# The last two tiles of an embedding's gate, multiplied before or after a conditional branch

## The chip, the cores and the metric

The kernel runs on one core of a Trainium2 chip. The core has five engines with instruction streams of their own: TensorE (PE: matrix products and transposes; PEld is its weight load), VectorE (DVE), ScalarE (ACT), GpSimd (POOL) and SyncE (SP), which here issues most of the DMA transfers. The metric is the time of one execution on the device, in microseconds (us). Before the change it is 3113.56 us, the median of 3 runs (3111.11 to 3114.87).

## The reference

The program computes two blocks one after the other on 512 tokens of 1024 features. The first block (attention, retention and a feed-forward network, with modulation) isn't touched. The second has two layers, and each ends with the part that matters here:

```python
for i in range(DEPTH):
    ...                                   # mixers, w_out
    h = layer_norm(DN_ALPHA * h + mix, ln1_g[i], ln1_b[i])
    y_moe = hier_moe(h, moe_wgc[i], moe_bgc[i], moe_wgf[i], moe_bgf[i],
                     moe_w1[i], moe_w3[i], moe_w2[i])
    y_ple = jax.nn.sigmoid(h @ ple_wg[i] + ple_bg[i]) * (p[i] @ ple_wp[i])
    h = layer_norm(DN_ALPHA * h + y_moe + y_ple, ln2_g[i], ln2_b[i])
```

`hier_moe` picks for each token one of 4 groups and 2 of its 4 experts; an expert is `(silu(t @ w1) * (t @ w3) * gate) @ w2` with 256 inner features. `y_ple`, the embedding, is a 1024 x 1024 product with a sigmoid, times a product of a 256-feature input `p`.

## The kernel before

Activations lie feature by feature: `x[:, m, token]` is feature tile m (128 features) of 512 tokens, and there are 8 tiles. Every product of full precision is made of three (`mm3`, L365): the weights and the activations are each split into a high part (ScalarE, L308) and a low part (VectorE, L309), and high x high, high x low and low x high are added up in one accumulator (L368, L369, L370). Weights are loaded by SyncE into stage slots (`stage`, L284) of two rings: `UPS` names the slots of the even pools, `DOWNS` those of the odd one.

`second_half` (L2648) is the end of a layer. The embedding's tiles 0 to 5 are multiplied and added early (`ple_g`, L2251, is the product, the sigmoid on ScalarE L2258 and the multiplication on VectorE L2259; `ple_add`, L2262, adds it to `ALPHA * x`, L2264). Then come the experts (`experts`, L2582). Tokens are gathered in blocks of 128: blocks 0 to 15 are the first 128 tokens of each expert, and blocks 16 to 22 take what experts have beyond that. For each block GpSimd gathers rows (`gather`, L2487), TensorE transposes them and multiplies up (`up`, L2540) and down (`down`, L2566); the result is evicted in two halves, by ScalarE (L2574) and VectorE (L2575), each scaled by the gate, and scattered by GpSimd to `ydram` (L2576). Which tokens a block beyond 16 holds is worked out by `list_further` (L2474): VectorE marks positions (L2373), TensorE multiplies (L2483), VectorE makes the indices (L2380 to L2387).

How many of blocks 17 to 22 are needed is known only at run time. `further` (L2616) loads the count into a register on every engine (L2618) and runs blocks 17 and 18 in an `If` (L2619), with blocks 19 to 22 in a second `If` inside it (L2621). A scheduler orders the instructions of each engine, but only within a stretch without branches: what is written before an `If` stays before it, what is written behind stays behind, on all engines. On a branch that isn't taken each engine counts what it has skipped, so that others who wait for it can go on.

Behind the branch SyncE loads the experts' results back token by token (`load`, L2628, 8 loads `rt`, L2636). `TokenNorm` (L712) makes the layer norm: `rows` (L715) transposes x to tokens (TensorE L722; copies ACT L726 and DVE L724), `tokens` (L729) adds the two loaded rows (L735, L736 with its sum), squares (ACT L738), takes the root on GpSimd (L384), scales (L743, two halves) and transposes back (TensorE L746, ACT L747). There are four token tiles t of 128; a half hf is 256 tokens, two of them. `gen` (L749) then makes the high and low parts of the new activations. In layer 0 the next layer's first projection (`Front.first`, L1859, tiles `wl`) follows, with panels loaded by `Front.panels` (L1855); in layer 1 the output is written.

In the kernel before, tiles 6 and 7 of the embedding (`ple(6, w67, UPS)`) and the list of block 17 (`list_further(1)`) are written behind block 16 and ahead of the branch.

Of the kernel before, what the change touches and what calls it, by code (L numbers as in the profile page):

```python
# [462 lines left out]
HS = (slice(0, 256), slice(256, 512))  # L463
# [248 lines left out]
class TokenNorm(LayerNorm):  # L712


    def rows(self, t):  # L715

        net, nc = self.net, self.net.nc
        X = self.pool.tile([128, D], F32, name=net.nm("xr"), tag="xr", bufs=4)
        for j in range(2):
# [3 lines left out]
            if j:  # L723
                nc.vector.tensor_copy(X[:, 512:], tr.rearrange("p m d -> p (m d)"))  # L724
            else:
                nc.scalar.activation(X[:, :512], tr.rearrange("p m d -> p (m d)"), AF.Copy)  # L726
        return X

    def tokens(self, t, X, r):  # L729

        net, nc, pool = self.net, self.net.nc, self.pool
        vt = nc.vector
        small = lambda tag: pool.tile([128, 1], F32, name=net.nm(tag), tag=tag, bufs=2)
        mean, var = small("tmean"), small("tvar")
        vt.tensor_tensor(X, X, r[0], op=OP.add)  # L735
        vt.scalar_tensor_tensor(X, X, 0.0, r[1], op0=OP.add, op1=OP.add, accum_out=mean)  # L736
        vt.tensor_scalar(mean, mean, -1.0 / D, None, op0=OP.mult)
        nc.scalar.activation(r[1], X, AF.Square, bias=mean, accum_out=var)  # L738
        vt.tensor_scalar(var, var, 1.0 / D, EPS2, op0=OP.mult, op1=OP.add)
        rstd = net.rsqrt(pool, var, 1)  # L740
        for j in range(2):
            cs = slice(512 * j, 512 * j + 512)
            vt.tensor_scalar(X[:, cs], X[:, cs], mean, rstd, op0=OP.add, op1=OP.mult)  # L743
            tr = self.sp.tile([128, 4, 128], F32, name=net.nm("tr"), tag="tr", bufs=2)
            for m in range(4):
                nc.tensor.transpose(tr[:, m], X[:, (4 * j + m) * 128:(4 * j + m + 1) * 128], net.ident)  # L746
            nc.scalar.activation(self.x[:, 4 * j:4 * j + 4, t * 128:(t + 1) * 128], tr, AF.Copy)  # L747
# [1444 lines left out]
UPS, DOWNS = slice(0, None, 2), slice(1, 2)  # L2192


class Moe:
# [34 lines left out]
    def small(self, name, *shape, dt=F32):  # L2230
        return self.mp.tile([128] + list(shape), dt, name=self.net.nm(name), tag="m_" + name)
# [253 lines left out]


    def gather(self, b):  # L2487
        if b >= 18:
            self.list_further(b - 16)
        xg = self.mp.tile([128, D], F32, name=self.net.nm("xg"), tag="xg", bufs=2)  # L2490
        self.net.nc.gpsimd.indirect_dma_start(out=xg, out_offset=None, in_=self.hd[:, :],
                                              in_offset=bass.IndirectOffsetOnAxis(ap=self.idx[:, b, 0:1], axis=0))
        return xg
# [147 lines left out]
def lnpools(net):  # L2641
    es = ExitStack()
    pool = es.enter_context(net.pool(net.nm("ln"), side="right"))
    sp = es.enter_context(net.pool(net.nm("ln_ps"), space=PSUM, side="right"))
    return es, pool, sp


def second_half(net, i, sides, hh, hl, lns, last):  # L2648

    moe = Moe(net, i, hh, hl)  # L2650
    pw = {m2: moe.ple_p(m2) for m2 in (0, 2)}
    pan = [net.cpanel(moe.wg[:, :, m2 * 128:m2 * 128 + 256], 8, 256) for m2 in (0, 2)]
    lt, sg = [], {}
    for hf in range(2):
        sides[hf].finish()
        if hf:
            lns.close()
            ms = ExitStack()
            ms.enter_context(net.more(0, 2))
        lt = moe.logits(hf)  # L2660
        for m in range(4):
            sg = moe.ple_g(m, pan[m // 2][m % 2], pw[m // 2 * 2][m % 2], HS[hf])
            if m == 0:
                moe.logits_t(hf, lt)
                moe.rows(hf)
                if hf:
                    router = net.side(moe.route())
            moe.ple_add(m, sg, HS[hf])
    full = slice(0, S)

    def ple(m2, w, some=slice(None)):
        g = net.cpanel(moe.wg[:, :, m2 * 128:m2 * 128 + 256], 8, 256, some=some)
        for mm in range(2):
            moe.ple_add(m2 + mm, moe.ple_g(m2 + mm, g[mm], w[mm], full), full)

    ple(4, moe.ple_p(4), UPS)
    w67 = moe.ple_p(6)
    moe.pes.close()
    ms.enter_context(net.more(0, 2))
    w0 = moe.first_weights()  # L2680
    net.finish(router)
    lists = moe.lists()

    with ms:
        def beside(e):
            for _ in range(2 if 3 <= e < 9 else 1):
                next(lists, None)

        blocks = [(e, e, (lambda e=e: beside(e))) for e in range(16)]
        moe.experts(blocks + [(16, moe.further_expert(0), None)], w0)  # L2690
        moe.list_further(1)
        ple(6, w67, UPS)
        moe.further()
    lns, pool, _ = lnpools(net)
    out = [TokenNorm(net, pool, moe.sp, net.x, hs, None if last else hh, hl, gname=f"l2g{i}", bname=f"l2b{i}") for hs in HS]
    pans = []
    rows = [moe.load(t) for t in range(4)]
    if not last:
        pans += Front.panels(net, i + 1, 512)
    X = [out[t // 2].rows(t) for t in range(4)]  # L2700
    for t in range(4):
        out[t // 2].tokens(t, X[t], rows[t])
        if t % 2:
            out[t // 2].start()
        if t == 3 and not last:
            pans += Front.panels(net, i + 1, 256)
    moe.es.close()
    return out, lns, pans


def second_block(net, stages, boundary):
# [15 lines left out]
    for i in layers:  # L2727
        front = Front(net, i, hh, hl)
        front.first(sides, pans)
        if i == 0:  # L2730
            net.tap("h_in0", net.x)
        lns.close()
        bs.close()
        front.second()
        front.mp2 = front.left.enter_context(net.pool(f"mixB{i}"))
        front.attention()
        bs.enter_context(net.more(3))
        lns, pool, sp = lnpools(net)
        sides = front.out_second(pool, sp, f"l1g{i}", f"l1b{i}")
        front.left.close()  # L2740
        if f"h1_{i}" in net.taps:
            for s in sides:
                s.finish()
            net.tap(f"h1_{i}", net.x)
        sides, lns, pans = second_half(net, i, sides, hh, hl, lns, i == layers[-1])
# [24 lines left out]
```

## Time and profile before

| what | us |
|---|---|
| median of 3 runs | 3113.56 |
| the profiled execution | 3106.33 |
| its span, first to last instruction | 3104.2 |
| layer 0: last block's down-products start | 2488.48 |
| layer 0: next layer's projection starts | 2526.86 |
| layer 1: last block's down-products start | 3060.32 |
| layer 1: last scaling starts | 3095.36 |

A row of a timeline gives the start from the span's begin, the duration, the engine, the line, the operation, the output and inputs by the program's names (without their numbers), the shape, how many instructions the row groups, and in brackets how long the engine was idle before and who released it. A name with a q (PEldq, DVEq) is an engine's queue, where branches and semaphores are handled. The granted clock (PEclk) is the share of TensorE's full clock that it was given.

### The profile page before, as it was taken

Reading aid. Unit: us, or ns where it says so; the run is one execution under the profiler, and the core shown is the slowest. Engines: PE = TensorE matmul, PEld = TensorE weight load, DVE = VectorE, ACT = ScalarE, POOL = GpSimd, SP = SyncE. Lnnn points to the kernel's source line nnn. Section 1 sums busy time; section 2 is a strip of 40 time slices with the busy share of each in tenths; the row PEclk is TensorE's granted clock in tenths of the full one; section 3 lists DMA queues with packets and bytes.
Section 4 is the critical chain, followed back from the end, with each engine's and each line's share of the span. In section 5 each row is a group of like instructions: output and inputs, shape, how many; then the busy total and the mean of one; then the engine's idle time right before and its main releaser. Section 6 shows DMA issues by size and latency. Waiting matters only on the chain. (4 is left out here: it accounts for less than half of the span.)

```text
span 3104.2 us, 42345 instructions
## 1 busy us (share of the span) xinstructions
PE 2939.8 (95%) x16384; PEld 2427.0 (78%) x16384; DVE 1902.0 (61%) x3557; ACT 1298.5 (42%) x2227; POOL 406.0 (13%) x389
## 2 busy tenths in 40 slices
PE   6999989999999999999999999999999988999995
PEld 5777779888888888888887788877876767787663
DVE  5566575545552664535465543669778766988865
ACT  3655563121212432323243322436555543656544
POOL 1112130000000200000020000221212212121220
PEclk8999999999999999999999999999999989999997
DMA  6121133324441222223133432231469944146993
GB/s 223 49 74 55 49 98 100 116 89 129 144 142 55 88 67 82 78 67 98 37 114 117 125 127 96 89 119 41 133 201 362 351 161 121 35 153 226 378 352 142
DMA packets 307875, 410.18 MB, mean 132 GB/s; under 512 B 16655, under 2 KB 248207, under 8 KB 307025
## 3 DMA queue, kind: packets, MB, share of 16 engines
q1 hardware_dynamic: 293840, 357.03, 35.0%
q0 software_dynamic: 13824, 50.34, 4.5%
q8 instruction: 133, 2.18, 0.3%
q14 instruction: 78, 0.63, 0.1%
HBM read 379.01 MB, written 28.31 MB: 131 GB/s over the span
## 5 line engine op out<-in xcount | busy, mean ns | idle before, releaser
L308 ACT ACTIVATE hi<-st 128x1024 fp32r<-128x1024 f32 (+1 forms) x420 | 432.7, 1034 | 691.9 <-PE ps L369 497.6
L309 DVE TENSOR_TENSOR lo<-st,hi 128x1024 fp32r<-128x1024 f32 (+1 forms) x420 | 510.5, 1219 | 233.9 <-ACT hi L308 222.5
L368 PE MATMUL ps<-hxh,hi 128*128 128x512 f32 (+1 forms) x1280 | 477.3, 374 | 2.5 <-DVE sg L828 0.8
L369 PE MATMUL ps<-hxl,hi 128*128 128x512 f32 (+1 forms) x1280 | 475.3, 372 | 0.5 <-DVE hxl L645 0.5
L370 PE MATMUL ps<-hxh,lo 128*128 128x512 f32 (+1 forms) x1280 | 475.0, 371 | 0.0
L368 PEld LDWEIGHTS ps<-hxh,hi 128*128 128x128 f32 x1280 | 241.9, 189 | 52.2 <-ACT sg L827 5.6
L370 PEld LDWEIGHTS ps<-hxh,lo 128*128 128x128 f32 x1280 | 242.0, 189 | 42.4 <-issue 1.2
L369 PEld LDWEIGHTS ps<-hxl,hi 128*128 128x128 f32 x1280 | 242.1, 189 | 41.2 <-issue 1.2
L368 PE MATMUL ps<-ah,hi 128*128 128x256 f32 (+1 forms) x592 | 200.5, 339 | 3.2 <-DVE x L774 1.6
L369 PE MATMUL ps<-al,hi 128*128 128x256 f32 (+1 forms) x592 | 198.5, 335 | 0.2 <-DVE al L378 0.2
L370 PE MATMUL ps<-ah,lo 128*128 128x256 f32 (+1 forms) x592 | 198.4, 335 | 0.0
L774 DVE SCALAR_TENSOR_TENSOR x<-ps,vecs,x 128x512 f32<-128x512 f32 (+1 forms) x136 | 84.4, 623 | 147.9 <-PE ps L370 147.8
L828 DVE TENSOR_TENSOR sg<-sg,ps 128x512 f32<-128x512 f32 (+1 forms) x70 | 40.1, 572 | 187.0 <-PE ps L370 186.3
L593 POOL TENSOR_TENSOR nacc<-nacc,nsq 128x256 f32<-128x256 f32 x56 | 49.4, 883 | 594.7 <-ACT nsq L592 593.5
L368 PEld LDWEIGHTS ps<-ah,hi 128*128 128x128 f32 x592 | 111.4, 188 | 19.0 <-DVE x L774 3.6
L2571 PE MATMUL py<-st,at 128*128 128x512 f32 x272 | 123.0, 593 | 1.7 <-DVE y L2575 1.2
L369 PEld LDWEIGHTS ps<-al,hi 128*128 128x128 f32 x592 | 111.5, 188 | 12.6 <-DVE al L378 0.4
L370 PEld LDWEIGHTS ps<-ah,lo 128*128 128x128 f32 x592 | 111.3, 188 | 12.6
L2545 PE MATMUL pa<-hi,xt 128*128 128x512 f32 x288 | 118.5, 412 | 0.5 <-ACT xt L377 0.5
L368 PE MATMUL ps<-hch,hi 128*128 128x256 f32 x416 | 117.7, 283 | 0.6 <-DVE mod L527 0.5
L369 PE MATMUL ps<-hcl,hi 128*128 128x256 f32 x416 | 117.2, 282 | 0.0
L370 PE MATMUL ps<-hch,lo 128*128 128x256 f32 x416 | 117.1, 282 | 0.0
(671 smaller groups left out, 7065.7 us busy)
## 6 DMA issues: line engine op xcount, KB each, us to landing
st<-moe_w_dram SPq DMA_DIRECT2D x136, 512.0 KB
st<-ffn_w_in_dram SPq DMA_DIRECT2D x44, 1024.0 KB
st<-moe_w_dram SPq DMA_DIRECT2D x34, 1024.0 KB
ast<-ada_w_dram SPq DMA_DIRECT2D x56, 512.0 KB
st<-ret_w_qkvg_dram SPq DMA_DIRECT2D x24, 1024.0 KB
st<-ffn_w_out_dram SPq DMA_DIRECT2D x24, 768.0 KB
st<-ada_w_dram SPq DMA_DIRECT2D x12, 1024.0 KB
st<-w_in_dram SPq DMA_DIRECT2D x12, 1024.0 KB
```

The costliest lines, as they stand in the source:

```text
L308: self.nc.scalar.activation(h, v, AF.Copy)
L309: self.nc.vector.tensor_tensor(l, v, h.bitcast(F32), op=OP.subtract)
L368: self.nc.tensor.matmul(ps, wh, xh, start=(i == 0), stop=False)
L369: self.nc.tensor.matmul(ps, wh, xl, start=False, stop=False)
L370: self.nc.tensor.matmul(ps, wl, xh, start=False, stop=(i == n - 1))
L593: nc.gpsimd.tensor_tensor(self.acc, self.acc, sq, op=OP.add)
L774: net.nc.vector.scalar_tensor_tensor(xm, p, self.gate[:, m:m + 1], xm, op0=OP.mult, op1=OP.add)
L828: nc.vector.tensor_tensor(sg, sg, pu, op=OP.mult)
L2545: nc.tensor.matmul(pa, th[:, k], wh, start=(k == 0), stop=False)
L2571: nc.tensor.matmul(py[:, n * 512:n * 512 + 512], at[:, f], w2[f][:, 0, n * 512:n * 512 + 512], start=(f == 0), stop=(f == 1))
```

## The change

The list of block 17 is made in `gather(17)`, so inside the branch, as the lists of blocks 18 to 22 already were. The gate weights of tiles 6 and 7 are loaded and split behind `further()`, and their products are made for each half of the tokens (256 columns) between the issue of the row loads and the transposes of that half. In layer 0 the load of the next layer's first two panels is written behind that instead of ahead of the transposes.

```diff
     def gather(self, b):
-        if b >= 18:
+        if b >= 17:
             self.list_further(b - 16)
...
         moe.experts(blocks + [(16, moe.further_expert(0), None)], w0)
-        moe.list_further(1)
-        ple(6, w67, UPS)
         moe.further()
+        g67 = net.cpanel(moe.wg[:, :, 768:1024], 8, 256, some=UPS)
     lns, pool, _ = lnpools(net)
...
     rows = [moe.load(t) for t in range(4)]
+
+    X = []
+    for hf, hs in enumerate(HS):
+        for mm in range(2):
+            moe.ple_add(6 + mm, moe.ple_g(6 + mm, g67[mm], w67[mm], hs), hs)
+        X += [out[hf].rows(t) for t in (2 * hf, 2 * hf + 1)]
     if not last:
         pans += Front.panels(net, i + 1, 512)
-    X = [out[t // 2].rows(t) for t in range(4)]
     for t in range(4):
         out[t // 2].tokens(t, X[t], rows[t])
```

The first place is SyncE's queue in layer 0. Before, ahead of the branch (`COMPARE_AND_BRANCH`), the panel of `ple_wg` stood among the down weights of the last blocks:

```order
L2515 DMA st_20962<-moe_w_2_dram 128x4x256
L284 DMA st_21115<-ple_wg_dram 128x8x256
L284 DMA st_20787<-moe_w_2_dram 128x2x1024
L284 DMA st_20871<-moe_w_2_dram 128x2x1024
L284 ISA
L284 DMA st_20965<-moe_w_2_dram 128x2x1024
L2619 COMPARE_AND_BRANCH
```

Three loads of weights and the whole branch stood behind it. Now, at the end of the same branch, it stands behind the branch's last instruction:

```order
L284 DMA st_21687<-moe_w_2_dram 128x2x1024
L2621 UNCONDITIONAL_BRANCH x2
L2619 UNCONDITIONAL_BRANCH
L284 DMA st_21814<-ple_wg_dram 128x8x256
L2636 DMA rt_21832<-ydram_18602 128x1024
L2636 DMA rt_21834<-ydram_18602 128x1024
```

It has moved past the branch, directly ahead of the eight row loads.

The second place is TensorE's queue at the start of that branch in layer 0. Before, the gate products of tiles 6 and 7 (`ps`, 512 columns) stood last ahead of the branch:

```order
L368 MATMUL ps_21154<-hxh_15866,hi_21121 128x512
L369 MATMUL ps_21154<-hxl_15867,hi_21121 128x512
L370 MATMUL ps_21154<-hxh_15866,lo_21122 128x512
L2618 TENSOR_LOAD exi_20375
L2619 COMPARE_AND_BRANCH
```

Now the last down-products (`py`) stand there:

```order
L2571 MATMUL py_21069<-st_20871,at_21039 128x512 x4
L2561 MATMUL tr_21078<-kident_69,act_21066 128x128 x2
L2571 MATMUL py_21083<-st_20965,at_21081 128x512 x4
L2618 TENSOR_LOAD exi_20375
L2619 COMPARE_AND_BRANCH
```

The gate products are gone from here; they stand behind the branch, after twelve of the transposes of L722.

The third place is VectorE's queue in the token stage of layer 0. Before, the low-part splits of the next layer's panels (`lo`) stood behind the last scaling (`nry_22050`, the fourth token tile):

```order
L758 TENSOR_SCALAR x<-x,vec 128x256
L739 TENSOR_SCALAR tvar_22044<-tvar_22044 128x1
L743 TENSOR_SCALAR xr_21955<-xr_21955,tmean_22043,nry_22050 128x512 x2
L309 TENSOR_TENSOR lo_21909<-st_21906,hi_21908 128x1024
L309 TENSOR_TENSOR lo_21913<-st_21906,hi_21912 128x1024
```

Now two of them stand between the two scalings of the first token tile (`nry_22033`), with the copies of later tiles, and ahead of the third tile's first sum (`L735`); two more stand ahead of the third tile's scaling:

```order
L2264 SCALAR_TENSOR_TENSOR x<-x,sg_21957 128x256
L737 TENSOR_SCALAR tmean_22026<-tmean_22026 128x1
L735 TENSOR_TENSOR xr_21919<-xr_21919,rt_21836 128x1024
L736 SCALAR_TENSOR_TENSOR xr_21919,tmean_22049<-xr_21919,rt_21838 128x1024
L2259 TENSOR_TENSOR sg_21986<-sg_21986,pw_19360 128x256
L739 TENSOR_SCALAR tvar_22027<-tvar_22027 128x1
L737 TENSOR_SCALAR tmean_22049<-tmean_22049 128x1
L2264 SCALAR_TENSOR_TENSOR x<-x,sg_21986 128x256
L743 TENSOR_SCALAR xr_21906<-xr_21906,tmean_22026,nry_22033 128x512
L724 COPY xr_21990<-tr_21997 128x512
L309 TENSOR_TENSOR lo_22019<-st_22016,hi_22018 128x1024
L724 COPY xr_22003<-tr_22010 128x512
```

Four low-part splits have moved ahead of the last scaling, and the multiplications and additions of the embedding's second half stand between the first two tiles' sums.

## Rows read from the trace of the kernel before

**Rows 1.** The page, first part: busy time of the engines over the span.
```profile
PE 2939.8 (95%) x16384; PEld 2427.0 (78%) x16384; DVE 1902.0 (61%) x3557; ACT 1298.5 (42%) x2227; POOL 406.0 (13%) x389
```

**Rows 2.** Chain of waits, 3060 to 3104: start, duration, what.
```profile
3073.77 6.78 DMA rt<-ydram
3080.65 1.23 DVE xr L735
...
3095.36 0.56 DVE xr L743
```

**Rows 3.** Timeline of TensorE, layer 0.
```profile
2488.48 3.60 PE L2571 MATMUL py<-st,at 128*128 128x512 f32 x8
...
2501.53 0.95 PE L722 MATMUL tr<-kident,x 128*128 128x128 f32 x7 [0.36 <-PEq L2619]
...
2526.86 0.56 PE L368 MATMUL wl<-hxh,hi 128*128 128x256 f32 x1
```

**Rows 4.** Timeline of VectorE, layer 0.
```profile
2486.27 0.69 DVE L2373 TENSOR_TENSOR P<-kiota,xkb 128x512 fp32r<-128x512 f32 x1
2486.88 0.75 DVE L2575 TENSOR_SCALAR y<-py,gate 128x512 f32<-128x512 f32 x1
...
2492.84 0.75 DVE L2575 TENSOR_SCALAR y<-py,gate 128x512 f32<-128x512 f32 x1 [4.16 <-ACT y L2574]
...
2505.53 1.22 DVE L735 TENSOR_TENSOR xr<-xr,rt 128x1024 f32<-128x1024 f32 x1
...
2521.22 0.41 DVE L758 TENSOR_SCALAR x<-x,vec 128x256 f32<-128x256 f32 x1 [0.19 <-ACT hxh L754]
...
2524.10 1.00 DVE L743 TENSOR_SCALAR xr<-xr,tmean,nry 128x512 f32<-128x512 f32 x2 [1.10 <-POOL nry L384]
2525.02 2.35 DVE L309 TENSOR_TENSOR lo<-st,hi 128x1024 fp32r<-128x1024 f32 x2
```

**Rows 5.** Timeline of ScalarE, layer 0.
```profile
2501.21 0.69 ACT L2258 ACTIVATE sg<-ps,vec 128x512 f32<-128x512 f32 x1 [2.83 <-PE ps L370]
...
2522.71 1.99 ACT L308 ACTIVATE hi<-st 128x1024 fp32r<-128x1024 f32 x2
```

**Rows 6.** Line L2619, the branch: count, durations in ns (min/median/max), first and last start.
```profile
L2619 DVEq COMPARE_BRANCH  x2: 55/64/72, 2497.9 to 3028.4; - x2
...
L2619 DVEq EVENT_SEMAPHORE  x1: 21/21/21, 2498.4 to 2498.4; - x1
```

**Rows 7.** Waits of SyncE's queue, 2440 to 2530: us in total, times, longest.
```profile
SPq L2636 <- DMA ydram<-y,idx: 16.3, 1, 16.3
...
SPq L2636 <- PEq L2619: 2.6, 1, 2.6
```

**Rows 8.** Timeline of SyncE: issues of 1 MB loads elsewhere.
```profile
1691.00 5.99 SPq L284 DMA_DIRECT2D st<-ffn_w_in_dram  x2
...
1809.12 0.37 SPq L284 DMA_DIRECT2D st<-ffn_w_in_dram  x1
```

**Rows 9.** Timeline of ScalarE: the splits that waited for those two loads.
```profile
1696.11 1.06 ACT L308 ACTIVATE hi<-st 128x1024 fp32r<-128x1024 f32 x1 [0.79 <-DMA st<-ffn_w_in_dram]
...
1819.36 1.06 ACT L308 ACTIVATE hi<-st 128x1024 fp32r<-128x1024 f32 x1 [6.24 <-DMA st<-ffn_w_in_dram]
```

**Rows 10.** Windows, layer 0: length, busy of each engine, granted clock, DMA share, GB/s.
```profile
2510.00:2514.00 4.00, 0.18 (x1) 0.18 (x2) 3.50 (x7) 0.48 (x2) 1.43 (x1) 0.51 1.02 412
...
2526.80:2531.00 4.20, 4.20 (x23) 4.20 (x23) 4.09 (x10) 4.05 (x8) 1.20 (x1) 0.56 0.67 238
2531.00:2552.90 21.90, 21.47 (x173) 20.54 (x173) 17.05 (x29) 9.86 (x16) 5.75 (x7) 1.00 0.44 141
```

**Rows 11.** Timeline of VectorE, layer 1.
```profile
3064.78 0.75 DVE L2575 TENSOR_SCALAR y<-py,gate 128x512 f32<-128x512 f32 x1 [4.51 <-ACTq L2621]
...
3076.16 1.23 DVE L735 TENSOR_TENSOR xr<-xr,rt 128x1024 f32<-128x1024 f32 x1 [5.66 <-DMA rt<-ydram]
```

**Rows 12.** Timeline of GpSimd, layer 1.
```profile
3035.03 0.95 POOL L2491 DMA_INDIRECT xg<-hdram,idx  x1 [8.21 <-issue]
...
3065.81 0.98 POOL L2576 DMA_INDIRECT ydram<-y,idx  x1 [4.28 <-DVEq L2621]
```

## The prediction

> **What bounds the kernel now.** I read the page first: over the whole span TensorE is the busiest engine and VectorE comes second [rows 1]. Such a share is a mean over stages and says nothing about the few microseconds that this change touches, so I went to the end of the expert stage of each layer of the second block. There are two such places and the work differs. In layer 0 the extra-block branch is skipped (its queue instructions pass through within a fraction of a microsecond [rows 6]); in layer 1 it is entered, since two more row gathers run there on GpSimd [rows 12].
>
> Layer 0, in the timeline of TensorE: the last block's eight down-products start at 2488.48, the first transpose of the token stage stands at 2501.53 and is released by TensorE's own passing of the branch, and the first projection of the next layer starts at 2526.86 [rows 3]. Between the first two TensorE is never idle: the gate products of feature tiles 6 and 7 fill it. Between the second and the third it mostly waits: VectorE runs the token sums from 2505.53 and its last scaling pair starts at 2524.10 [rows 4]. So after the branch the chain is VectorE, ScalarE and GpSimd in turn, and TensorE only follows. After 2526.86 TensorE is dense again [rows 10], so whatever makes that start late moves the rest of the kernel. Layer 1, in the chain of waits: it ends with the row load (6.78 us), the token sums and the last scaling at 3095.36 [rows 2], and then the output. What comes late there is late in the end.
>
> **The edit of the load, both layers.** In the old order the 1 MB panel of gate weights for tiles 6 and 7 was issued among the weights of the last blocks, its split was long finished, and its 48 products of 512 columns stood beside the last down-products. In the new order the load is the first thing that SyncE issues behind the branch. It goes into a stage slot that the skipped experts use too, so it waits until VectorE and ScalarE have counted the branch. That such waits are real here, two rows show: the row loads waited 2.6 us for nothing but TensorE's passing of the same branch [rows 7], and in layer 1 the last down-product's eviction waits behind ScalarE's passing of the inner one [rows 11]. So the load starts only when the last eviction is through, and then a load, a split, 96 products of 256 columns, two sigmoid-and-add steps and the transposes follow one another, where before there was only a transpose.
>
> Layer 0, step by step:
> - The second list's work leaves the path: its 0.69 us step stands in front of block 15's eviction on VectorE (2486.27, then 2486.88 to 2487.63 [rows 4]), and block 16's products start 0.85 after that eviction [rows 3]. Without the list and the gate products between, I take 1.2 us for the start; at least 0, at most 0.85 + 0.69 = 1.5.
> - Block 16's eviction on VectorE then starts at 2492.84 - 1.2 = 2491.6 and ends at 2492.4 [rows 4]. The branch was counted at 2498.4, 0.5 us after VectorE came to it [rows 6]: 2492.9 for the issue of the load.
> - A 1 MB load: issued 1691.00 in pieces of a pair, read by ScalarE at 1696.11 [rows 8, 9]: 5.1 us. Upper bound from a load beside other traffic: 1809.12 to 1819.36, 10.2 us [rows 8, 9]. Few other transfers run at that moment, so I take 5.1: 2498.0.
> - Two splits on ScalarE are 1.99 us [rows 5]. Products can start after the first, at 2499.05. TensorE will have been idle since its few early transposes; after the last ones in the old trace the granted clock of 2510 to 2514 is 0.51, that is the lower level, 1.2 GHz, and it is 0.56 in the first 4.2 us after the restart, in which 23 products of 256 columns fit; later 173 fit in 21.47 us busy, 0.124 each, at 2.4 GHz [rows 10]. Half 0 has 48 products: 4.2 + 25 x 0.124 = 7.3 us, to 2506.35.
> - Sigmoid (0.69 for 512 columns [rows 5], so that is a ceiling), multiplication and addition at 0.41 for 256 columns [rows 4] and hand-overs: 1.75 us, to 2508.1. The last transposes, about 0.4, and two copies at 0.69 (what a 512-wide step costs [rows 4]): the first token sum at 2509.9 instead of 2505.53, **+4.4**.
> - From there to the end of the last scaling took 2524.10 + 1.00 - 2505.53 = 19.6 us [rows 4]. New on VectorE inside it: four half-wide steps for the second half, 4 x 0.41 = 1.6, and four low-part splits of the next layer's panels, which stood behind the last scaling at 2525.02, 2 x 2.35 = 4.7 [rows 4]; on ScalarE two more sigmoids and four high-part splits (4.0 [rows 5]) stand ahead of the third and fourth squares. Floor 0 (all of it falls into waits for GpSimd), ceiling 6.3 + 4.0 + 1.4 = 11.7 (one after another). The low-part splits alone exceed the idle time of VectorE that I see there, so I take the middle, **+6**.
> - TensorE's projection then starts near 2537.3 instead of 2526.86 and runs as before: layer 0 costs **+10.4**. Ends: 4.4 alone and 4.4 + 11.7 = 16.
>
> By the Trainium skill's page "DMA: Bandwidth & Descriptors", section "Anatomy of one DMA — SWDGE (gpsimd) path", a transfer costs about 2.0 us plus its bytes over 436 GB/s, which for 1 MB makes an estimate of 4.4 us; the trace's 5.1 [rows 8, 9] is longer, and by the page the two loads together would cost 1.4 us less.
>
> Layer 1, in the same manner. Both extra lists now stand in the branch and no gate products come before them on TensorE. The second gather, at 3035.03 [rows 12], comes earlier by up to 4.8 us, but the blocks' weights land at about that time too, so of this 0 to 4.8 reaches the last scatter (3065.81 [rows 12]); I take 2.8. The last eviction then ends at 3062.7 [rows 11], the branch is counted at 3063.2, the panel is there at 3068.3, and the same steps (1.05 + 7.3 + 1.75 + 1.8) give a first token sum at 3080.2 instead of 3076.16, **+4.0**. That sum waited 5.66 us for the row load [rows 11], so the load's wait goes and the gate products take its place: the rows are there by then. Behind it four half-wide steps are added (1.6), and a short wait for the third row load (it was released at 3080.65 by the 6.78 us load [rows 2]) goes: **+1.0**. No next panels are split here. Layer 1 costs **+5.0**, ends 1 and 9.
>
> Sum: 10.4 + 5.0 = 15.4. The profiled execution took 3106.33, so 3121.7; it lies 7.2 under the median of the runs, and to that I carry the difference: **3129**.
>
> A rule that speaks against the change: the Trainium skill's "TensorE: Matmul & The Clock Gate", section "HAM oscillation — how this bites in real kernels", says that a TensorE that waits for a transfer starts each tile at the low clock again. In the old trace the waits after the branch show just such a drop [rows 10]; with the high clock throughout, half 0 would be 48 x 0.124 = 6.0 instead of 7.3, and the sum 2.6 lower.
>
> **Rivals.**
> - The load isn't held by the branch, since its slot was free long ago, and is hidden as before. Then products start with TensorE's passing near 2491, warm, and the row loads bound: they need the last scatter's landing, which moves 1.2 earlier, and lose the 2.6 of waiting for TensorE [rows 7]. Layer 0: -3.5 + 6 = +2.5, layer 1: -2.8 + 1.0 = -1.8; 3114.5. Against it: the waits on the branch [rows 7, 11].
> - Not slower but faster: the same, and the panel splits and half-wide steps fall wholly into VectorE's waits for GpSimd. Then only the gains are left, -3.5 and -2.8: **3107**. It decides if the load is issued before VectorE reaches the branch. For it: there are such waits in the token stage [rows 2]. Against it: the same rows as above, and the low-part splits, which were on nobody's path at 2525.02 and now stand in it.
> - Worse: the load shares the queues with the row loads and the scatter and takes 10.2 us as at 1809.12 [rows 8, 9], in both layers: +10.2, 3139. For it: the row loads are issued right behind it. Against it: the load comes first in the queue.
>
> **How the numbers follow.** Forecast 0.70, load hidden 0.10, faster 0.08, worse 0.12. The forecast's own range from the ends of its terms that don't all fall together is 3120 to 3138. What a measurement of this kernel can tell from no change is about 0.2%, 6.2 us: bounds 3107.3 and 3119.8. Hidden loads lie inside them, the faster case on the lower one; of the forecast a little (both layers at their lower ends) falls inside. Faster 0.07, same 0.14, slower 0.79. For the range I reach to the hidden load and to the worse one: 3113 to 3138.
>
> **What would show it.** Right: in layer 0 the panel's load issued near 2493, with ScalarE waiting for it to about 2498; TensorE idle for some 5 us before the gate products and at the low clock in their first part; the first token sum near 2510 and the last scaling ending near 2535 (both against unchanged starts of block 16); in layer 1 the chain of waits running over the panel's load and the gate products instead of the row load. Wrong: the load issued before 2485, or the first token sum waiting for row loads; then the forecast's main term is gone. If the token stage takes 19.6 us as before although the splits stand in it, the second term is gone, and 3123 is left.

## The result and the profile after

The changed kernel takes 3134.31 us (median of 4 runs, 3131.08 to 3139.85) against 3112.34 of the kernel before on the same chip: ratio 1.0074, interval 1.0061 to 1.0087, so 19 to 27 us slower. The forecast was slower, 3129 in a range of 3113 to 3138; of the difference it had 15.4 us where 22 were measured. The profiled execution of the changed kernel took 3133.86 us, 27.5 more than that of before; some 3 of these lie in stages that the change doesn't touch, so below I compare stretches between two events, not times from the start.

SyncE's queue in layer 0, from its timeline and its waits (2460 to 2540), and GpSimd's last scatter, from its timeline:

```profile
2494.21 0.38 SPq L284 DMA_DIRECT2D st<-ple_wg_dram  x1
2502.39 4.38 SPq L2636 DMA_DIRECT2D rt<-ydram  x8
```

```profile
SPq L284 <- DVEq L2619: 10.8, 1, 10.8
```

```profile
2493.93 0.96 POOL L2576 DMA_INDIRECT ydram<-y,idx  x1 [4.30 <-DVE y L2575]
```

The load of the panel (the 1 MB of gate weights for tiles 6 and 7) is issued 0.6 us behind the last eviction on VectorE, and what it waited for is VectorE's passing of the branch: the step on which the forecast rested. ScalarE, VectorE and TensorE behind it, each from its timeline:

```profile
2501.36 2.00 ACT L308 ACTIVATE hi<-st 128x1024 fp32r<-128x1024 f32 x2 [3.96 <-DMA st<-ple_wg_dram]
```

```profile
2487.64 0.75 DVE L2575 TENSOR_SCALAR y<-py,gate 128x512 f32<-128x512 f32 x1
2492.90 0.75 DVE L2575 TENSOR_SCALAR y<-py,gate 128x512 f32<-128x512 f32 x1 [4.51 <-ACT y L2574]
2502.45 2.36 DVE L309 TENSOR_TENSOR lo<-st,hi 128x1024 fp32r<-128x1024 f32 x2 [8.79 <-ACT hi L308]
...
2512.56 0.42 DVE L2264 SCALAR_TENSOR_TENSOR x<-x,sg 128x256 f32<-128x256 f32 x1
...
2514.61 1.21 DVE L735 TENSOR_TENSOR xr<-xr,rt 128x1024 f32<-128x1024 f32 x1
...
2538.90 1.00 DVE L743 TENSOR_SCALAR xr<-xr,tmean,nry 128x512 f32<-128x512 f32 x2 [0.44 <-POOL nry L384]
```

```profile
2483.28 3.60 PE L2571 MATMUL py<-st,at 128*128 128x512 f32 x8
...
2488.44 3.70 PE L2571 MATMUL py<-st,at 128*128 128x512 f32 x8 [1.34 <-DVE y L2575]
...
2502.47 0.58 PE L368 MATMUL ps<-hxh,hi 128*128 128x256 f32 x1 [4.33 <-ACT hi L308]
...
2541.37 0.56 PE L368 MATMUL wl<-hxh,hi 128*128 128x256 f32 x1
```

Read it from the eviction of block 15 (2487.64; before 2486.88 [rows 4]): to the first token sum it takes 26.97 us, before 18.65, so **+8.3**; from there to the next layer's projection 26.76, before 21.33 [rows 3, 4], so **+5.4**. VectorE is idle for 8.79 us ahead of the panel's low-part split (2502.45), where before it already added tiles 6 and 7. In layer 1, from the timelines of SyncE, ScalarE and VectorE:

```profile
3080.45 0.40 SPq L284 DMA_DIRECT2D st<-ple_wg_dram  x1
```

```profile
3088.34 2.00 ACT L308 ACTIVATE hi<-st 128x1024 fp32r<-128x1024 f32 x2 [8.80 <-DMA st<-ple_wg_dram]
```

```profile
3034.33 0.75 DVE L2575 TENSOR_SCALAR y<-py,gate 128x512 f32<-128x512 f32 x1
...
3079.57 0.75 DVE L2575 TENSOR_SCALAR y<-py,gate 128x512 f32<-128x512 f32 x1 [4.51 <-ACTq L2621]
3089.43 2.36 DVE L309 TENSOR_TENSOR lo<-st,hi 128x1024 fp32r<-128x1024 f32 x2 [9.11 <-ACT hi L308]
...
3101.61 2.35 DVE L735 TENSOR_TENSOR xr<-xr,rt 128x1024 f32<-128x1024 f32 x2
```

Block 15's eviction of layer 1 in the kernel before, from VectorE's timeline:

```profile
3017.58 0.75 DVE L2575 TENSOR_SCALAR y<-py,gate 128x512 f32<-128x512 f32 x1
```

The last eviction comes 45.24 after block 15's (47.20 before: -2.0); from it to the first token sum are 22.04 us, before 11.38 [rows 11], **+10.7**; and from there to the end of the span (3132.1) 30.49, before 28.04, +2.4. The sum no longer waits for the row load, as it did for 5.66 us [rows 11]: the gate products are what is late. The terms add up to 24.8; with the 3 us that lie ahead of block 15 in the two layers, that is what the spans of the profiled pair differ by (27.9).

The load, which the forecast priced at 5.1 us after one of two loads elsewhere [rows 8, 9], took 7.15 us in layer 0 and 7.89 in layer 1. The windows of the changed kernel show TensorE's granted clock before and in the products of the first half (columns as in [rows 10]):

```profile
2494.00:2497.00 3.00, 1.96 (x10) 1.35 (x10) 0.00 (x0) 0.80 (x2) 0.89 (x1) 0.69 0.41 95
2497.00:2501.00 4.00, 0.69 (x2) 0.29 (x2) 0.00 (x0) 0.40 (x1) 0.00 (x0) 0.50 0.91 324
2502.40:2508.50 6.10, 5.88 (x26) 5.59 (x27) 2.36 (x2) 2.24 (x3) 0.00 (x0) 0.50 0.85 275
2508.50:2512.00 3.50, 3.50 (x30) 3.50 (x30) 0.85 (x2) 0.88 (x2) 0.00 (x0) 0.96 0.99 379
```

TensorE had done ten transposes in 2494 to 2497, in which the granted clock fell (0.69), and no more than two in 2497 to 2501. It stayed at half its clock (1.2 GHz) for 6.1 us after it started; I had taken over the 4.2 us of [rows 10].

### The profile page after: what moved, and what is told of

It reads as the page before. It is cut to its first block, busy times and chain, and to the rows that moved or that the text cites. A ratio compares the mean times of both kernels' runs of the same rounds, so it can differ in the third digit from the quotient of the medians.

```text
span 3132.1 us, 42536 instructions
## 1 busy us (share of the span) xinstructions
PE 2948.3 (94%) x16472; PEld 2438.7 (78%) x16472; DVE 1900.0 (61%) x3557; ACT 1296.5 (41%) x2228; POOL 408.5 (13%) x389
## 5 line engine op out<-in xcount | busy, mean ns | idle before, releaser
L368 PE MATMUL ps<-hxh,hi 128*128 128x512 f32 (+1 forms) x1312 | 486.7, 372 | 15.4 <-ACT hi L308 12.3
L369 PE MATMUL ps<-hxl,hi 128*128 128x512 f32 (+1 forms) x1312 | 483.7, 369 | 0.6 <-DVE hxl L645 0.6
L370 PE MATMUL ps<-hxh,lo 128*128 128x512 f32 (+1 forms) x1312 | 481.5, 368 | 0.0
L368 PEld LDWEIGHTS ps<-hxh,hi 128*128 128x128 f32 x1312 | 251.0, 192 | 65.0 <-ACT hi L308 13.9
L369 PEld LDWEIGHTS ps<-hxl,hi 128*128 128x128 f32 x1312 | 251.5, 192 | 40.2 <-issue 1.2
L370 PEld LDWEIGHTS ps<-hxh,lo 128*128 128x128 f32 x1312 | 250.8, 191 | 40.7 <-issue 0.7
L370 PE MATMUL ps<-ah,lo 128*128 128x256 f32 (+1 forms) x592 | 198.4, 335 | 0.0
L370 PEld LDWEIGHTS ps<-ah,lo 128*128 128x128 f32 x592 | 111.3, 188 | 12.6
L2545 PE MATMUL pa<-hi,xt 128*128 128x512 f32 x288 | 118.7, 412 | 0.5 <-ACT xt L377 0.5
L2546 PE MATMUL pa<-hi,xt 128*128 128x512 f32 x288 | 117.1, 407 | 0.0
L370 PE MATMUL ps<-hch,lo 128*128 128x256 f32 x416 | 117.1, 282 | 0.0
## 6 DMA issues: line engine op xcount, KB each, us to landing
st<-moe_w_dram SPq DMA_DIRECT2D x34, 1024.0 KB, 10.5
```

The source lines that it names most:

```text
L368: self.nc.tensor.matmul(ps, wh, xh, start=(i == 0), stop=False)
L369: self.nc.tensor.matmul(ps, wh, xl, start=False, stop=False)
L370: self.nc.tensor.matmul(ps, wl, xh, start=False, stop=(i == n - 1))
L2545: nc.tensor.matmul(pa, th[:, k], wh, start=(k == 0), stop=False)
L2546: nc.tensor.matmul(pa, tl[:, k], wh, start=False, stop=False)
```

## The experiments

Each ratio is against the kernel before, run on the same chip. "Stretch" means: in layer 0 from block 15's eviction to the first token sum, before 18.65, changed 26.97.

**The list alone.** The kernel before with

```diff
-        if b >= 18:
+        if b >= 17:
-        moe.list_further(1)
```

> The kernel before with only the list of block 17 moved into the branch; tiles 6 and 7 stay ahead of it. Theory A (the late load and what hangs on it cost everything): 0 to -3 us against before, since block 16's products start up to 1.2 us earlier in layer 0 and the gate products still cover. Rival B (the list in the branch delays block 17's gather in layer 1, and this is part of the cost): +3 to +6 us, first gather of layer 1 3 us later after the last eviction of block 16.

1.0014 (1.0004 to 1.0024), 3 us slower: near B, and not what A said. Layer 0 gains 0.4 us in its stretch (18.22). In layer 1 GpSimd gathers block 17 at 3040.78, 12.2 us after the last eviction of block 16, before 2.3:

```profile
3029.61 0.96 POOL L2576 DMA_INDIRECT ydram<-y,idx  x1 [4.32 <-DVE y L2575]
3040.78 1.28 POOL L2491 DMA_INDIRECT xg<-hdram,idx  x1 [10.21 <-PE lst L2483]
```

It waits for the list's products, which stand on TensorE behind the gate products of tiles 6 and 7. Block 15's eviction to the last one takes 49.28 instead of 47.20.

**Tiles 6 and 7 alone.** The changed kernel with

```diff
-        if b >= 17:
+        if b >= 18:
+        moe.list_further(1)
         moe.further()
```

> The changed kernel with the list of block 17 put back ahead of the branch; tiles 6 and 7 stay behind it. Theory A: as slow as the changed kernel or a little slower, +22 to +25 us against before. Rival B (the list carries part of the cost): +16 to +19 us.

1.0064 (1.0050 to 1.0078): the changed kernel's interval overlaps, so the list's share is not told from nothing there. The stretch in layer 0 is 26.94. Nearly all of the cost is in the tiles; with them gone from in front, no cost of the list in the branch can be told: block 15's eviction to the last one takes 45.56 in layer 1 here and 45.24 in the changed kernel.

**The next layer's panels loaded first.** The changed kernel with `pans += Front.panels(net, i + 1, 512)` moved back directly behind `rows = ...`.

> The changed kernel with the next layer's first two panels loaded ahead of the gate products, as they were placed before. Theory A with my term of 6 us for the panel splits in the token chain of layer 0: splits go back or move in front of the first sum, where VectorE waits for the gate products; -4 to -6 us against the changed kernel, so +16 to +18 against before. Rival C (the splits stand in idle time): no difference, +22. Rival D (1 MB loads ahead of the gate panel's landing or the row loads cost more than the splits): slower than the changed kernel by 2 us or more.

1.0073 (1.0055 to 1.0090), no difference. This tells less than I wanted: the scheduler put the splits into VectorE's queue at almost the same places, and the stretch and the token stage are the same to 0.1 us (26.90, 26.77). Where that line is written doesn't matter here.

**The panel loaded ahead of the branch.** The changed kernel with

```diff
-    ms.enter_context(net.more(0, 2))
+    ms.enter_context(net.more(0, 1))
+    net.st_rings = net.st_rings + [(None, 0)]
+    ms.enter_context(net.more(0, 1))
...
+        own = net.st_rings[-1][0].tile([128, 2048], F32, name=net.nm("st"), tag="st", bufs=1)
+        own = own.rearrange("p (k c) -> p k c", k=8)
+        net.nc.sync.dma_start(own, moe.wg[:, :, 768:1024])
+        net.st_rings = net.st_rings[:-2]
         moe.further()
-        g67 = net.cpanel(moe.wg[:, :, 768:1024], 8, 256, some=UPS)
+        g67 = [net.split(own[:, :, j:j + 128]) for j in (0, 128)]
```

> The changed kernel with only the raw load of the gate panel issued ahead of the branch, into a slot that the branch's experts do not use (they have 3 slots instead of 4 for their up weights); the split and the products stay behind the branch. Theory A (the load is held by the branch and stands on the path): the split starts when ScalarE passes the branch, some 8 us earlier in each layer, so about -16 us against the changed kernel, +5 to +8 against before; the last scatter of layer 0 lands in about 3.4 us again instead of 7.0. Rival E (the row loads bound as well, the load is hidden beside them): -4 us or less against the changed kernel, VectorE's first token sum then waits for rt.

0.9986 (0.9977 to 0.9995): 4 us faster than before and 27 faster than the changed kernel. ScalarE and VectorE in layer 0, from their timelines:

```profile
2488.35 2.01 ACT L308 ACTIVATE hi<-st 128x1024 fp32r<-128x1024 f32 x2 [1.44 <-DVEq L2619]
```

```profile
2481.68 0.75 DVE L2575 TENSOR_SCALAR y<-py,gate 128x512 f32<-128x512 f32 x1
2486.94 0.75 DVE L2575 TENSOR_SCALAR y<-py,gate 128x512 f32<-128x512 f32 x1 [4.51 <-ACT y L2574]
...
2499.90 2.35 DVE L735 TENSOR_TENSOR xr<-xr,rt 128x1024 f32<-128x1024 f32 x2
```

The split now waits for the branch, not for a load; the stretch is 18.22, and in layer 1 the last eviction to the first sum is 13.46 instead of 22.04. That is A. But more was gained than A had, and block 15's eviction comes at 2481.68 instead of 2487.64, before any of this: the slot edit did something of its own (below). TensorE, whose products here wait for the branch and the split but not for a load, starts them at the low clock too and leaves it sooner than after 6.1 us, as the windows of this run show:

```profile
2489.40:2491.40 2.00, 1.94 (x8) 1.81 (x9) 1.96 (x2) 1.98 (x4) 0.00 (x0) 0.50 0.65 262
2491.40:2493.40 2.00, 2.00 (x17) 2.00 (x16) 0.40 (x1) 0.74 (x1) 0.00 (x0) 0.86 0.00 0
```

**One layer at a time.** The change made for `i == 0` or for `i == 1` only, the other layer as before.

> The change made in layer 0 alone, layer 1 as before. By the intervals of the trace of the changed kernel (last eviction but one to the first token sum +8.3, first sum to the next layer's projection +5.4) theory A expects +12 to +14 us against before. Rival F (the delay of the projection is given back later in layer 1, which has slack): +5 or less.

> The change made in layer 1 alone. By the intervals of the trace (branch -2.0, last eviction to the first token sum +10.7, from there to the end +2.4) theory A expects +9 to +12 us against before, and the two layers alone add up to the whole change, +22 to +25. My prediction had 5 for this layer; that rival would show +4 to +6.

Layer 0: 1.0035 (1.0022 to 1.0049), 11 us: near A's 12 to 14, which the interval (7 to 15 us) holds, and not given back later. Layer 1: 1.0012 (1.0004 to 1.0021), 4 us, on the side of my forecast's 5, though its trace shows +6.5 from block 15's eviction to the end (86.62 to 93.16) and that of the full change +11.2. Together 0.47% against 0.74% for the whole; the upper ends of the two add up to 0.70%, the lower end of the whole is 0.61%, so that the layers add up is neither shown nor excluded. In the trace of the layer-1 kernel the first sum comes 19.31 after the last eviction and of the full one 22.04. The panel's load took 6.18 us there, from SyncE's and ScalarE's timelines, instead of 7.89:

```profile
3067.36 0.40 SPq L284 DMA_DIRECT2D st<-ple_wg_dram  x1
```

```profile
3073.54 2.00 ACT L308 ACTIVATE hi<-st 128x1024 fp32r<-128x1024 f32 x2 [7.09 <-DMA st<-ple_wg_dram]
```

The first half's products and additions took 9.5 us instead of 10.5; the two make the 2.7. Layer 1 differs by such amounts from trace to trace: from block 15's eviction to the end it takes 94.3 us in the panels-first run and 94.2 in the run with later panels (below), which leave layer 1 as it is in the changed kernel, against 97.8 in the changed kernel. So the trace of the changed kernel shows a long layer 1. Why the load's time varies there isn't shown.

**Panels loaded later.** The changed kernel with the 512-column panels requested at the third token tile, beside the others.

> The changed kernel with the next layer's first two panels loaded behind the third token tile, so that their four low-part splits stand later in VectorE's queue (three of them right around the last two scalings, one behind). Theory G (the splits in the token chain of layer 0 cost the 5.4 us between the first sum and the projection): -3 to -5 us against the changed kernel, and that interval back at 22 to 24. Rival H (the half-wide steps and the gate products of the second half cost it): no change in that interval, or slower because the panels land late.

1.0067 (1.0055 to 1.0079), no difference that can be told. The first sum to the projection takes 25.11 instead of 26.76: 1.7 of the 5.4 us. Only one of four splits got behind the last scaling. VectorE between the sums and the scalings, from its timeline:

```profile
2529.58 1.22 DVE L735 TENSOR_TENSOR xr<-xr,rt 128x1024 f32<-128x1024 f32 x1
2534.14 1.22 DVE L309 TENSOR_TENSOR lo<-st,hi 128x1024 fp32r<-128x1024 f32 x1
2535.40 1.21 DVE L309 TENSOR_TENSOR lo<-st,hi 128x1024 fp32r<-128x1024 f32 x1
2537.05 1.00 DVE L743 TENSOR_SCALAR xr<-xr,tmean,nry 128x512 f32<-128x512 f32 x2 [0.44 <-POOL nry L384]
```

So G holds for a small part; the rest of the 5.4 stays unassigned between the half-wide steps and ScalarE's queue, where the third square (2533.17) now stands behind five high-part writes:

```profile
2530.72 2.55 ACT L754 ACTIVATE hxh<-x,vec 128x256 fp32r<-128x256 f32 x5
2533.17 1.14 ACT L738 ACTIVATE rt<-xr,tmean 128x1024 f32<-128x1024 f32 x1
```

(that is the changed kernel).

**The last scatter doubled.** The changed kernel with a second scatter of the last block's result, into a scratch tensor, behind the first.

> The changed kernel with the last block's scatter made twice in each layer, the second time into a tensor of its own that nobody reads, so twice the scatter traffic stands beside the panel's load. Theory K (the load takes 7.1 and 7.9 us instead of 5.1 because it shares the DMA queues with the last scatter): the load takes 1.5 us or more longer in each layer, and the kernel is 3 to 6 us slower than the changed one. Rival L (the load is slow by itself at this place, by its issue or by the branch): load unchanged at 7 to 8 us, kernel within 2 us of the changed one, unless the row loads become the bound (first token sum then released by rt).

1.0078 (1.0063 to 1.0092). The load took 7.35 and 7.83 us (2501.47 to 2508.82, 3087.83 to 3095.66), and the kernel is within 2 us of the changed one, both as L said. But the second scatter was issued at 2502.45, 1.3 us behind the first, and landed 7.6 us later, so most of it may have moved behind the load. The run doesn't decide.

**The last scatter taken away.** The changed kernel with block 15's result (block 17's in layer 1) scattered a second time to the rows of the last block, whose own result is then not scattered:

```diff
+        last = 16 if self.i == 0 else 18
+        if b == last:
+            return
...
+        if b == last - 1:
+            st = nc.gpsimd.indirect_dma_start(out=self.yd[:, :], in_=y, in_offset=None,
+                                              out_offset=bass.IndirectOffsetOnAxis(ap=self.idx[:, last, 1:2], axis=0))
```

> The changed kernel with the last block's scatter taken away from behind the last eviction: the result of the block before it is scattered a second time, to the last block's rows, and the last block's own result is not scattered, so these rows hold other numbers. Theory K (the panel's load is slow because it shares the queues with that scatter): the load takes 5.0 to 5.8 us in both layers instead of 7.1 and 7.9; the kernel 3 to 5 us faster than the changed one. Rival L (slow by itself at this place): 7 to 8 us as before, kernel within 2 us.

1.0047 (1.0029 to 1.0065), 4 us faster than the changed kernel by the medians, though the intervals just overlap. SyncE and ScalarE in layer 0:

```profile
2501.72 0.38 SPq L284 DMA_DIRECT2D st<-ple_wg_dram  x1
```

```profile
2506.78 2.00 ACT L308 ACTIVATE hi<-st 128x1024 fp32r<-128x1024 f32 x2 [1.56 <-DMA st<-ple_wg_dram]
```

The load takes 5.06 us there, what it took at 1691.00 [rows 8, 9], against 7.04 to 7.56 in the seven traces in which the last scatter starts with it in layer 0: K holds in layer 0. In layer 1 it takes 6.40, above K's 5.8 and no less than the 6.18 of the layer-1 kernel, which has the scatter beside it; the seven traces with the scatter have 6.18 to 9.01 there. So for layer 1 K isn't shown. The scatter pays too in layer 0; its landing, from the DMA views of before, of the changed kernel and of the early load, in this order:

```profile
ydram<-y,idx POOLq DMA_INDIRECT x1, 3.4
```

```profile
ydram<-y,idx POOLq DMA_INDIRECT x1, 7.0
```

```profile
ydram<-y,idx POOLq DMA_INDIRECT x1, 3.3
```

**The two slots alone.** The kernel before with only the first three lines of the early load's edit: one pool of two stage slots becomes two pools of one.

> The kernel before with one edit only: the pool of the last two stage slots is made of two pools of one slot each, as in the kernel with the early load. Theory M (the early-load kernel gains some 5 us elsewhere, since its profile reaches the last blocks of layer 0 at 2481.7 instead of 2487 to 2490; that comes from the slots, not from the load): -4 to -7 us against before, last evictions of layer 0 near 2482. Rival N (that was the scatter between executions, or belongs to the load): within 2 us of before.

0.9978 (0.9967 to 0.9989), 7 us faster than before and the fastest of all kernels here: M. SyncE at the start of layer 0's experts, of this kernel and of before:

```profile
2278.43 1.06 SPq L2515 DMA_DIRECT2D st<-moe_w_dram  x2
2299.43 0.92 SPq L2515 DMA_DIRECT2D st<-moe_w_dram  x2
```

```profile
2280.51 0.45 SPq L284 DMA_DIRECT2D st<-moe_w_dram  x1
2301.98 24.07 SPq L2515 DMA_DIRECT2D st<-moe_w_dram  x14
```

With one pool, all further up weights wait 21.0 us for a product `ps` of L370 (`SPq L2515 <- PE ps L370` in the waits). The last one that ends before the wait does is of the embedding's input `pT`, from TensorE's timeline of before:

```profile
2301.56 0.39 PE L370 MATMUL ps<-pT,lo 128*128 128x512 f32 x1
```

It is made for tiles 6 and 7, and the pool that holds `pT` is closed right ahead of the slots' pool in the program, so that the slots can take over its region. With two pools, two loads go out ahead of that wait. The first expert's eviction (ScalarE's half) comes at 2321.46 instead of 2327.32. The early-load kernel, 0.9986, can't be told from this one: with the load ahead of the branch, tiles 6 and 7 behind it cost nothing that these runs show, and gain nothing.

**The changed kernel with the two slots.** The changed kernel with those three lines only.

> The changed kernel with the last two stage slots in pools of one slot each and nothing else, so the early-load kernel without the early load. Theory A: the slots give their 7 us here too, so +14 to +17 us against before, and the early load alone is then worth the difference to the early-load kernel, 18 to 22 us. Rival N (slots and late load are not independent; the early-load kernel owed more to the slots): +8 us or less.

1.0064 (1.0051 to 1.0078), 3 us better than the changed kernel by the medians, but the intervals overlap, and less than the 7 expected, though its first eviction too is early (2324.3 against 2328.5). What this run is for is the pair with the early load, which differs from it in the load and its slot alone: 1.0064 against 0.9986, 24 us, by the ends of the intervals 17 to 31. A had 18 to 22.

**Load and split ahead of the branch.** The changed kernel with the panel split ahead of the branch into two buffer pairs in a pool of their own, the panels loaded later, and the two slots.

> The changed kernel with the gate panel loaded and split ahead of the branch into a pair of buffers of its own, products behind the branch, the next layer's first two panels loaded behind the third token tile, and the two slots in pools of their own. Theory A: no load and no split on the path; in layer 0 the first token sum comes 16 to 18 us after the last eviction but one (18.65 before), then bound by the row loads; 24 to 27 less than the changed kernel. If M holds as well, -5 to -10 us against before, the fastest so far. Rival H (gate products and half-wide steps in the token stage cost more than the cover they give): 0 to +4 against before.

1.0035 (1.0022 to 1.0047), 7 to 15 us: not the fastest, and outside of what A and H said. The first sum comes hardly earlier (18.01), since VectorE now waits for the row loads ahead of it:

```profile
2499.41 0.69 DVE L724 COPY xr<-tr 128x512 f32<-128x512 f32 x1 [3.23 <-DMA rt<-ydram]
```

The token stage takes 26.02, and the stretch from the projection to block 15's eviction in layer 1 502.1 instead of 490.7 to 495.7 in the others. That stretch uses the buffer pairs whose pool I had cut; the run mixes too much to say more.

## Why the prediction was right, and where it fell short

- The load is held by the branch: right, shown by its issue at 2494.21 with the wait on VectorE's passing (predicted 2492.9 with block 15 0.8 us earlier), and by the early load, which gives back 24 us. The rivals "not held" and "faster" are out. Of the two rows that I leaned on, the one of layer 1 [rows 11] proves little: in layer 0 of the changed kernel, ahead of any branch, the same eviction idles the same 4.51 us, for ScalarE's half. The -3.5 in these rivals should read -3.8 (1.2 + 2.6), which changes no chance.
- Its price of 5.1 us was mis-sized: 7.15 and 7.89. I had written that few other transfers run at that moment, and named row loads as the competitor. The last scatter runs then; it is issued within 0.3 us of the load, and taken away it gives the load back its 5.06 in layer 0. The rival "worse" named the scatter too, but leaned on the row loads, which are issued only when the load has landed (2502.39 against the split at 2501.36). Missing: 2.05 in layer 0, shown, and 2.8 in layer 1, where the cause stays open.
- The half's products and what follows: 7.3 + 1.75 predicted, 10.5 measured (2502.47 to 2512.98), 1.5 too few in each layer, since the low clock lasted 6.1 us and not 4.2; 4.2 was one restart's value. The Trainium skill's rule from "TensorE: Matmul & The Clock Gate", section "HAM oscillation — how this bites in real kernels", that a wait for a transfer makes the next products cold, agrees with this trace (0.50). But the clock had fallen already behind the wait for the branch (0.69 in 2494 to 2497), and the early load, whose products wait for no transfer, starts at 0.50 as well.
- These two make the first sums late by 7.9 (against 4.4; both from block 15's products, 2482.08 before and 2483.28 after) in layer 0 and by 10.7 instead of 6.8 from the last eviction in layer 1.
- The token stage of layer 0: 6 predicted, 5.4 measured. The size is right, but the reason only in part: moving splits away brought 1.7.
- Layer 1's branch: -2.8 predicted, -2.0 measured, and the end +2.4 instead of +1.0. The whole layer costs 11.1 by this trace, 6.5 by the trace of the layer-1 kernel and 4 (1 to 7) by its runs: 2.7 of the difference between the two traces are the load and the products, and the rest lies behind the first sum and isn't resolved.
- The list in the branch: taken as a gain in both layers. The 1.2 us came in layer 0 (block 16's products start 5.16 behind block 15's, before 6.40), but two thirds of them come without the list's move (5.60). Beside the tiles' move it gives 0.4 us there and 0.3 in layer 1's branch by the traces, less than the runs can tell; alone it costs 3 us.
- Nearly all of these errors of size point one way: the terms of the trace add up to 24.8 against 15.4. The time stays within the ends of the forecast's own terms (3120 to 3138).

## What to carry to other kernels

Before work is moved behind a branch, ask which of its loads share slots with the branch's body: here such a load started only when VectorE had passed the branch (a wait of 10.8 us), and a megabyte that was hidden before stood on the path, in layer 0 beside a scatter that slowed it from 5.06 to 7.15 us. Products put behind the branch started at the low clock (0.50), whether they waited for the load or not. And look at what the first loads of a pool of several slots wait for: with one pool per slot two of them went out 21 us earlier, and the kernel was 7 us faster (0.9978).

## What the runs showed of the hardware that I had not expected

In the changed kernel a 1 MB load and a 0.5 MB scatter issued within 0.3 us of each other took 7.15 and 7.0 us, where without the other they took 5.06 and 3.4 (layer 0; in layer 1 the load took 6.18 to 9.01 us beside the scatter and 6.40 without). TensorE's low clock lasted 6.1 us after the start of the products at 2502.47 in the changed kernel; after the restart of [rows 10] the granted clock was 0.56 over 4.2 us, and in the early load it was 0.50 over the first 2 us and 0.86 over the next 2.
